# Hybrid gMLP and linear-attention layer on one core: the sample's attention in scaled two-byte halves, keys turned by DMA, states held at chunk ends, z and q/k weight steps and output steps moved a slot

## The chip, the core and the metric

The kernel runs on one core of a Trainium2 chip. Its engines are TensorE (PE, matmuls, with PEld for the loading of weights), VectorE (DVE), ScalarE (ACT), GpSimd (POOL) and SyncE (SP, here the queue that issues the DMAs). Each engine works through its own instructions in the order in which the program wrote them, and waits for the others through semaphores. The metric is device time in microseconds (us) of one launch; lower is better.

## The reference, cut to what matters

Two sequences, a prompt of 512 tokens and a sample of 2048, go through the same layer of width 1024. The part that this change touches is `gla_direction`, called once forward and once on the flipped sequence:

```python
h = rmsnorm(x, norm_pre)
u_a, v_a, z_a, q_b, k_b, v_b, z_b, lr_f, lr_b = split(h @ w_in)
out_a = spatial_gating(gelu(u_a), gelu(v_a), w_sp, b_sp, g_v_a) * silu(z_a)
# per direction, in chunks: g = log_sigmoid(lr @ w_gk + b_gk) / 16
bcum = cumsum(g, axis=2); b_last = bcum[:, :, -1:]
q_in, k_in = q * exp(bcum), k * exp(-bcum)
scores  = where(mask, einsum('bnchd,bnjhd->bnhcj', q_in, k_in), 0)
o_intra = einsum('bnhcj,bnjhe->bnche', scores, v)
chunk_kv = einsum('bnjhd,bnjhe->bnhde', k * exp(b_last - bcum), v)
state = exp(b_last) * state + chunk_kv            # scanned over the chunks
o_inter = q_in @ state_before
out_b = rmsnorm(o_fwd + o_bwd, g_norm_b) * silu(z_b)
y = x + rmsnorm(concat(out_a, out_b) @ w_out, norm_post)
```

The kernel uses chunks of 128 tokens; "chunk g" below is one of 20 such chunks, 0 to 3 of the prompt and 4 to 19 of the sample.

## The kernel before

Tokens are taken in five **blocks** of 512: block 0 is the prompt, blocks 1 to 4 the sample. A block is a row of **slots**. Each slot issues one projection of the block's normed input `hT` (a [128 x 512] result in one PSUM bank), and around it the steps of other generators whose turn it is. A projection is 24 matmuls, since input and weights are split into a high and a low float16 half and three of the four products are kept. In a sample block the slots are 0 to 3 `pv`, 4 to 7 `pzb`, 8 to 11 `pvb`, 12 to 15 `pqk` (columns 0, 2, 1, 3, so two of q and two of k), and 16 to 23 `pu` and `pz` in turn. In block 0 `pv` is done earlier, and slots 0 to 3 are `pzb`, 4 to 7 `pvb`, 8 to 11 `pu`, 12 to 15 `pqk`, 16 to 19 `pz`. After block 4 comes the **output stage**: for each of 20 row tiles two groups `py` of 24 matmuls with `w_out` and one small group `oi` (q times the state).

The program's order is final: nothing reorders it. In `slot`, the steps come in this order: the projections' readers (`mains`), weight steps named in `pre`, `early`, `aux` (the generators that a table adds at a slot), then the slot's own projection, then what was put into `late` (small matmuls). The PSUM pool `pj` of the projections has two banks, so the projection of slot s+2 waits until everything that reads the result of slot s is done.

What the change and the prediction name:

- **Weights** come as float32 `raw_*` and are split by `split_k`: ACT writes the high half, DVE the low half. For `w_z` four steps of two splits stand in block 0. Before them `g_wprep` takes a bound: two transposes on PE (`bank_z <- ident, m_z`), a DVE maximum `m_z`, and a small matmul with a row of ones (L191) that gives it to all partitions.
- **Next block's input**: `g_xprep` loads 128 rows `x`, squares them on ACT (L119), writes high half on ACT (L138) and low half on DVE (L140) and turns both by DMA into `hT` (L129). Its x and xs tiles share two buffers.
- **Gates**: `g_gates` makes the decay factors `QE` and `KE` with DVE scans (L576), a subtraction on each of POOL and DVE (L582, L584), a copy `ab` (L586, L587) and the exponentials on ACT.
- **v**: `g_vb` evacuates `pvb` with one ACT copy (L475). **q, k**: `g_qk` multiplies `pqk` into `QE` and `KE` with four DVE instructions.
- **Attention of a chunk**: `g_gla` computes scores `X` (forward) and `Y` (backward), merges them into `pr`, turns the keys into `kt` (on PE as `ktr` for chunks 0 to 3, 18, 19, else with 16 32-wide DVE transposes), and then `kv = kt^T v` and `o = pr^T v`, four float32 matmuls each. The forward state `U` is carried here.
- **Output steps**: `g_out` (called as `out_step(t)`) loads a row tile `L` of scratch, carries the backward state `U`, does `oi`, normalizes and splits into `OT`. `g_wout` loads and splits a piece of `w_out`.

Of the kernel before, what the change touches and what calls it, by code (L numbers as in the profile page):

```python
# [16 lines left out]
P = 128  # L17
# [3 lines left out]
NB = 5  # L21
# [10 lines left out]
OS = 2.0 ** 14  # L32


@with_exitstack
def tile_hybrid_gmlp_gla(ctx: ExitStack, tc: tile.TileContext, x_prompt, x_sample, norm_pre, w_in,
# [195 lines left out]
    def g_wprep(name):  # L232
# [126 lines left out]
    cols = cp.tile([P, 48], F32, name="cols")  # L359
# [182 lines left out]
    def g_gates(b):  # L542
# [64 lines left out]


    def decay_row(rows, g):
        n = rows.stop - rows.start  # L610
        return wst[rows, g, :].rearrange("p (h o) -> p h o", o=1).to_broadcast([n, H, P])

    PE_TR = (0, 1, 2, 3, 18, 19)

    def g_gla(b, i):
        g = 4 * b + i
        first = g in (0, 4)
        f, r = slice(0, 64), slice(64, 128)
# [4 lines left out]
        on_pe = g in PE_TR  # L623
        tr = pt.tile([P, H, P], F32, name=f"ktr{g}", tag="tr") if on_pe else None

        def k_transpose(q):
            d = slice(32 * q, 32 * q + 32)
            for c in range(4):
                nc.vector.transpose(out=kt[32 * c:32 * c + 32, :, d],  # L629
                                    in_=KE[b][d, :, i * P + 32 * c:i * P + 32 * c + 32])  # L630

        def mm():
            for h in range(H):
                nc.tensor.matmul(X[:, h, :], lhsT=KE[b][f, h, tk], rhs=QE[b][f, h, tk], start=True, stop=True)  # L634
                nc.tensor.matmul(Y[:, h, :], lhsT=KE[b][r, h, tk], rhs=QE[b][r, h, tk], start=True, stop=True)
            if on_pe:
                for h in range(H):
                    nc.tensor.transpose(tr[:, h, :], KE[b][:, h, tk], ident)
# [8 lines left out]
        if on_pe:  # L647
            nc.scalar.activation(kt, tr, AF.Copy)
        else:
            k_transpose(2)  # L650
            k_transpose(3)
# [9 lines left out]
        def kv_mm():  # L661
            for h in range(H):
# [488 lines left out]
```

## Time and profile before

| what | value |
|---|---|
| three runs | 976.3, 976.66 and 977.02 us; median 976.66 |
| the profiled execution | 976.77 us, of which the span of the trace is 975.1 |
| PE busy | 958.1 us, 98% of the span |
| DVE, ACT, POOL busy | 575.8 (59%), 417.9 (43%), 212.4 (22%) |

An engine's busy time is the union of its instructions. PE's matmuls overlap one another, so what a group of them costs is read from the start of its first to the start of what comes next, and not from the duration shown. The granted clock is full in every slice of the page.

### The profile page before, as it was taken

To read this page: it belongs to the slowest core of one execution; us is meant where nothing else is said; L and a number is where in the kernel's file an instruction comes from. 1 tells how busy PE (TensorE), PEld (TensorE's weight loads), DVE (VectorE), ACT (ScalarE), POOL (GpSimd) and SP (SyncE) were. 2 spreads that over 40 slices of the span, in tenths; PEclk is the share of its full clock that TensorE was granted. 3 is DMA by queue.
4 is the path that set the end of the run, shared out by engine and by line. 5 is a ranking of instruction groups with operands and counts; after the bars stand their busy time and mean duration, and the time that the engine had idled before them with its cause. 6 is when DMAs were issued, how large, how long until landed. Compare 5 with 4: busy or idle time off the path is not lost. (4 is left out here: it accounts for less than half of the span.)

```text
span 975.1 us, 14265 instructions
## 1 busy us (share of the span) xinstructions
PE 958.1 (98%) x5485; PEld 504.8 (52%) x5485; DVE 575.8 (59%) x1105; ACT 417.9 (43%) x792; POOL 212.4 (22%) x258
## 2 busy tenths in 40 slices
PE   8999999999999999999999999999999999999997
PEld 7744446544465544456444556444556555555454
DVE  6765864456756645755655667564665655565553
ACT  6778743535224363224453242343144444344341
POOL 1030203312021312011311112221022332222220
PEclk9999999999999999999999999999999999999999
DMA  9612134232433121333121331021416788767842
GB/s 322 229 68 84 24 106 121 86 97 44 97 108 109 44 87 44 87 119 105 50 74 44 108 120 66 33 76 66 151 66 202 223 263 252 221 221 228 251 158 97
DMA packets 113668, 120.71 MB, mean 124 GB/s; under 512 B 62784, under 2 KB 86208, under 8 KB 111040
## 3 DMA queue, kind: packets, MB, share of 16 engines
q1 hardware_dynamic: 113600, 119.80, 39.6%
q8 instruction: 43, 0.70, 0.3%
q14 instruction: 25, 0.20, 0.1%
HBM read 69.44 MB, written 36.70 MB: 109 GB/s over the span
## 5 line engine op out<-in xcount | busy, mean ns | idle before, releaser
L372 PEld LDWEIGHTS <-hT 128*128 128x128 f16 x1344 | 130.3, 98 | 159.1 <-issue 5.6
L836 PE MATMUL py<-wo,OT 128*128 128x512 f16 (+1 forms) x960 | 207.9, 376 | 0.0
L836 PEld LDWEIGHTS <-OT 128*128 128x128 f16 x984 | 96.3, 98 | 106.9
L372 PE MATMUL pzb<-w_zb,hT 128*128 128x512 f16 x480 | 106.6, 379 | 1.2 <-DVE tb L466 1.2
L382 PE MATMUL pz<-hT,w_z 128*128 128x512 f16 x480 | 107.0, 379 | 0.1
L382 PE MATMUL pu<-hT,w_u 128*128 128x512 f16 x480 | 106.6, 379 | 0.0
L372 PE MATMUL pvb<-w_vb,hT 128*128 128x512 f16 x480 | 104.9, 379 | 1.0 <-DVE tb L466 1.0
L382 PE MATMUL pqk<-hT,w_qk 128*128 128x512 f16 x480 | 104.8, 379 | 0.0
L629 DVE STREAM_TRANSPOSE kt<-KE 32x128 f32<-32x128 f32 x224 | 67.8, 303 | 34.4 <-PE kv L663 31.4
L372 PE MATMUL pv<-w_v,hT 128*128 128x512 f16 x384 | 84.5, 379 | 0.4 <-ACT vf L398 0.4
L382 PEld LDWEIGHTS <-w_u 128*128 128x128 f16 x480 | 46.9, 98 | 56.4
L382 PEld LDWEIGHTS <-w_qk 128*128 128x128 f16 x480 | 46.8, 98 | 56.0
L441 POOL TENSOR_TENSOR th<-th,gu 128x512 f32<-128x512 f32 x20 | 32.7, 1637 | 195.8 <-DVE th L440 195.8
L382 PEld LDWEIGHTS <-w_z 128*128 128x128 f16 x480 | 45.7, 98 | 54.2 <-issue 0.2
L455 ACT ACTIVATE th<-t 128x512 f32<-128x512 f32 x20 | 12.6, 630 | 132.2 <-DVE t L454 132.2
L855 DVE TENSOR_TENSOR y<-py,npost 128x512 f32<-128x512 f32 (+1 forms) x40 | 27.4, 685 | 70.7 <-PE py L836 60.6
L852 ACT ACTIVATE junk<-py 128x512 f16<-128x512 f32 (+1 forms) x40 | 23.7, 591 | 85.8 <-DVE y L855 84.6
L466 DVE SCALAR_TENSOR_TENSOR tb<-tb,pzb 128x512 f32<-128x512 f32 x20 | 13.7, 686 | 56.9 <-ACT tb L465 56.9
L582 POOL TENSOR_TENSOR KE<-QE 64x1024 f32<-64x1024 f32 x10 | 32.1, 3209 | 63.3 <-DVE QE L576 40.4
L486 DVE SCALAR_TENSOR_TENSOR QE<-pqk,ev_qk,QE 64x512 f32<-64x512 f32 x40 | 30.0, 749 | 26.0 <-PE pqk L382 24.3
L119 ACT ACTIVATE xs<-x 128x1024 f16<-128x1024 f32 x16 | 16.8, 1051 | 64.5 <-DMA x<-in_x_sample_dram 29.1
L646 DVE COPY_PREDICATED pr<-jlec,X 128x512 f32<-128x512 int32 x20 | 14.6, 730 | 40.6 <-ACT pr L645 40.5
(307 smaller groups left out, 1352.1 us busy)
## 6 DMA issues: line engine op xcount, KB each, us to landing
L<-scr SPq DMA_DIRECT2D x20, 1280.0 KB, 6.7
out_dram<-y SPq DMA_DIRECT2D x19, 512.0 KB, 7.4
x<-in_x_sample_dram SPq DMA_DIRECT2D x16, 512.0 KB, 4.0
xres<-in_x_sample_dram SPq DMA_DIRECT2D x16, 512.0 KB, 8.2
scr<-tb SPq DMA_DIRECT2D x20, 256.0 KB, 2.0
scr<-QE SPq DMA_DIRECT2D x20, 256.0 KB, 3.1
scr<-t SPq DMA_DIRECT2D x20, 256.0 KB, 2.4
scr<-S SPq DMA_DIRECT2D x20, 256.0 KB, 2.0
```

The costliest lines, as they stand in the source:

```text
L119: nc.scalar.activation(junk, xt, AF.Square, accum_out=ms)
L372: nc.tensor.matmul(ps, lhsT=hT[b][:, k, a, i * P:(i + 1) * P], rhs=w[:, k, c, :], start=(n == 0), stop=(n == 3 * KC - 1))
L382: nc.tensor.matmul(ps, lhsT=w[:, k, c, col:col + P], rhs=hT[b][:, k, a, :], start=(n == 0), stop=(n == 3 * KC - 1))
L441: nc.gpsimd.tensor_tensor(t, t, gus[b, h], op=ALU.mult)
L466: nc.vector.scalar_tensor_tensor(th, th, 1.0, ps, op0=ALU.add, op1=ALU.mult)
L486: nc.vector.scalar_tensor_tensor(o, ps[64 * hh:64 * hh + 64, :], s[64 * d:64 * d + 64], o, op0=ALU.mult, op1=ALU.mult)
L582: nc.gpsimd.tensor_tensor(Mv[64:128, h:h + 2], Av[64:128, h:h + 2, :, ::-1], mid[64:128, h:h + 2].to_broadcast([64, 2, 4, P]), op=ALU.subt ...
L629: nc.vector.transpose(out=kt[32 * c:32 * c + 32, :, d], in_=KE[b][d, :, i * P + 32 * c:i * P + 32 * c + 32])
L646: nc.vector.copy_predicated(pr, C["jmask"], X)
L836: nc.tensor.matmul(bank[:, cs], lhsT=OT[:, k, a, :], rhs=wo[n][:, k, c, cs], start=(m == 0), stop=(m == 3 * KC - 1))
L852: nc.scalar.activation(junk[:, cs], pss[j][:, cs], AF.Square, accum_out=ms[:, n + j:n + j + 1])
L855: nc.vector.tensor_tensor(y[:, n * 512:(n + 1) * 512][:, cs], pss[j][:, cs], npost[n][:, cs], op=ALU.mult)
```

## The change

- For the sample's chunks (4 to 19) `vb`, the keys and the masked scores are kept as a high and a low float16 half, and `kv` and `o` become three float16 matmuls per head (24 per chunk in place of 8 float32 ones).
- The keys of a chunk are first brought to the chunk's end (`kb`, on POOL), split (ACT and DVE), and turned by two DMA transposes on SP. The DVE and PE transposes of these chunks go.
- The scores get a scale per block: `g_qk` squares `pqk` on ACT, and a new `g_scores` sums this over partitions with two PE transposes and a matmul with ones (`bank_s`).
- `vb` is written by ACT (high) and by DVE (low), both from PSUM.
- States are held at chunk ends: one more POOL multiplication per chunk, and one (`um`) per row tile of the output stage for 15 tiles.
- In block 0 the four `w_z` steps go from slots 12 to 15 into slots 13 to 16, and one step of `w_z`'s bound from slot 11 to 12. The bound of `w_qk` is taken in two halves.
- The four `w_out` pieces of block 3 go to block 4, slots 5, 6, 12, 13, and the other four from slots 12 to 15 to 14 to 17. The output steps of block 4 are in other slots.

The diff, cut to its core:

```diff
@@ g_vb
+        if b > 0:
+            if i == 0:
+                vb[b] = bp.tile([P, 4, 2, 512], F16, name=f"vb{b}", tag="big8")
+            hi = vb[b][:, i, 0, :]
+            nc.scalar.activation(hi, ps, AF.Copy, scale=KS)
+            nc.vector.scalar_tensor_tensor(vb[b][:, i, 1, :], ps, KS, hi, op0=ALU.mult, op1=ALU.subtract)
+            return
@@ g_qk
+        if b > 0:
+            sq = tp.tile([P, BT], F32, name=f"sqk{b}_{c}", tag="S")
+            nc.scalar.activation(sq, ps, AF.Square, scale=SQ, accum_out=sqk[:, c:c + 1])
+def g_scores(b):
+        m = sp.tile([P, 2], F32, name=f"msc{b}", tag="s_msc", bufs=1)
+        nc.vector.tensor_reduce(m, sqk.rearrange("p (a c) -> p a c", a=2), axis=AX.X, op=ALU.add)
+        bank = pt.tile([P, 512], F32, name=f"bank_s{b}", tag="tr")
...
+                nc.tensor.transpose(bank[0:1, j * P:(j + 1) * P], m[:, j:j + 1], ident)
...
+        late.append(lambda: nc.tensor.matmul(bank[:, 256:258], lhsT=ones1, rhs=m2, start=True, stop=True))
@@ g_gla, sample chunks
+        nc.gpsimd.tensor_tensor(kb.rearrange("p (h t) -> p h t", t=P), KE[b][:, :, tk],
+                                spread(ab[:, 1], all_p, g), op=ALU.mult)
...
+        nc.scalar.activation(prh, Y, AF.Copy)
+        nc.scalar.activation(kb16[:, 0, :], kb, AF.Copy)
+        nc.vector.copy_predicated(prh, C["jmask"], X)
+        nc.vector.tensor_tensor(kb16[:, 1, :], kb, kb16[:, 0, :], op=ALU.subtract)
+        for a in range(2):
+            nc.sync.dma_start_transpose(out=kt16[:, a, :].rearrange("p (h d) -> p h d", d=P), in_=kb16[:, a, :])
...
+        nc.scalar.activation(pr16[:, 0, :], pr, AF.Copy, scale=s)
+        nc.vector.scalar_tensor_tensor(pr16[:, 1, :], pr, s, pr16[:, 0, :], op0=ALU.mult, op1=ALU.subtract)
...
+            for out, w in ((kv, kt16), (o, pr16)):
+                for h in range(H):
+                    hs = slice(h * P, (h + 1) * P)
+                    for n, (a, c) in enumerate(((0, 0), (0, 1), (1, 0))):
+                        nc.tensor.matmul(out[:, h, :], lhsT=w[:, a, hs], rhs=vb[b][:, i, c, hs],
+                                         start=(n == 0), stop=(n == 2))
@@ g_out
+            if b > 0:
+                mid = tp.tile([P, H, P], F32, name=f"um{g}", tag="ot")
+                nc.gpsimd.tensor_tensor(mid[r], U[r], to_mid(r, g), op=ALU.mult)
@@ block 0
-    tiny = {0: ["vb"], 1: ["vb"], 2: ["u"], 3: ["u"], 5: ["qk", "sp"], 6: ["qk", "sp"], 10: ["z"], 11: ["z"]}
-    pre = {2: [("vb", 4)], 3: [("vb", 5)], 12: [("z", 2)], 13: [("z", 2)], 14: [("z", 2)], 15: [("z", 2)]}
+    tiny = {0: ["vb"], 1: ["vb"], 2: ["u"], 3: ["u"], 5: ["qk", "sp"], 6: ["qk", "sp"], 10: ["z"], 12: ["z"]}
+    pre = {2: [("vb", 4)], 3: [("vb", 5)], 13: [("z", 2)], 14: [("z", 2)], 15: [("z", 2)], 16: [("z", 2)]}
@@ blocks 1 to 4
+        at(16, g_scores(b))
...
-            for s, piece in zip((19, 20, 21, 22), wo_pieces):
-                at(s, g_wout(*piece))
...
-            for s, piece in zip((12, 13, 14, 15), wo_pieces[4:]):
+            for s, piece in zip((5, 6, 12, 13, 14, 15, 16, 17), wo_pieces):
```

Two places show how the order of instructions moves. The number behind a name is a running number of the tile. The first place is ACT at the end of block 0, from the decay exponentials on: `w_z` are the high halves of the z weights, two per row, and `xs_1`, `xs_2` are rows of the next block's input. Before:

```order
L594 ACTIVATE KE_971<-KE_971 128x2048
L596 ACTIVATE ab<-ab 128x2x16
L218 ACTIVATE w_z<-raw_z,nps_z 128x512 x2
L119 ACTIVATE xs_1_1314,xms_1_1315<-x_1_1277 128x1024
L218 ACTIVATE w_z<-raw_z,nps_z 128x512 x2
L138 ACTIVATE xs_1_1314<-x_1_1277,xms_1_1315 128x1024
L218 ACTIVATE w_z<-raw_z,nps_z 128x512 x2
L119 ACTIVATE xs_2_1391,xms_2_1392<-x_2_1353 128x1024
L138 ACTIVATE xs_2_1391<-x_2_1353,xms_2_1392 128x1024
```

And now:

```order
L617 ACTIVATE KE_974<-KE_974 128x2048
L619 ACTIVATE ab<-ab 128x2x16
L220 ACTIVATE w_z<-raw_z,nps_z 128x512 x2
L121 ACTIVATE xs_1_1313,xms_1_1314<-x_1_1266 128x1024
L220 ACTIVATE w_z<-raw_z,nps_z 128x512 x2
L140 ACTIVATE xs_1_1313<-x_1_1266,xms_1_1314 128x1024
L220 ACTIVATE w_z<-raw_z,nps_z 128x512 x2
L121 ACTIVATE xs_2_1390,xms_2_1391<-x_2_1352 128x1024
L220 ACTIVATE w_z<-raw_z,nps_z 128x512 x2
L140 ACTIVATE xs_2_1390<-x_2_1352,xms_2_1391 128x1024
```

The last pair of splits, rows 6 and 7 of the eight slices of `w_z`, stood ahead of the square of `xs_2` and now stands behind it.

The second place is DVE in block 2 while PE does the four `pvb` projections; `tb_3` belongs to the last `pzb`, `KE`, `QE` and `ab` to the gates. Before:

```order
L466 SCALAR_TENSOR_TENSOR tb_3_3348<-tb_3_3348,pzb_3_3322 128x512
L575 TENSOR_TENSOR KE_3203<-QE_3202,KE_3203 128x1024
L576 SCALAR_TENSOR_TENSOR QE_3202<-smask,KE_3203 128x1024
L575 TENSOR_TENSOR KE_3203<-QE_3202,KE_3203 128x1024
L576 SCALAR_TENSOR_TENSOR QE_3202<-smask,KE_3203 128x1024
L584 TENSOR_TENSOR KE_3203<-QE_3202 64x2048
L586 COPY ab<-QE_3202 128x4x4
L587 TENSOR_TENSOR ab<-QE_3202 128x4x4
L140 SCALAR_TENSOR_TENSOR xs_1_3317<-x_1_3285,xms_1_3318,xs_1_3317 128x1024
```

And now:

```order
L598 TENSOR_TENSOR KE_3267<-QE_3266,KE_3267 128x1024
L599 SCALAR_TENSOR_TENSOR QE_3266<-smask,KE_3267 128x1024
L491 SCALAR_TENSOR_TENSOR vb_3444<-pvb_0_3418,vb_3444 128x512
L598 TENSOR_TENSOR KE_3267<-QE_3266,KE_3267 128x1024
L599 SCALAR_TENSOR_TENSOR QE_3266<-smask,KE_3267 128x1024
L607 TENSOR_TENSOR KE_3267<-QE_3266 64x2048
L609 COPY ab<-QE_3266 128x4x4
L610 TENSOR_TENSOR ab<-QE_3266 128x4x4
L142 SCALAR_TENSOR_TENSOR xs_1_3381<-x_1_3349,xms_1_3382,xs_1_3381 128x1024
L491 SCALAR_TENSOR_TENSOR vb_3444<-pvb_1_3457,vb_3444 128x512
L491 SCALAR_TENSOR_TENSOR vb_3444<-pvb_2_3485,vb_3444 128x512
L491 SCALAR_TENSOR_TENSOR vb_3444<-pvb_3_3516,vb_3444 128x512
```

The low half of the first `pvb` is read between the two scans, and that of the second only behind the whole gate chain and the input's low half. Block 3 has the same order; in block 4 there is no `xs_1`; in block 1 `vb` of the first three stands ahead of the second scan.

## Rows read from the trace of the kernel before

**Rows 1.** The page, busy time (share) x instructions of each engine.
```profile
PE 958.1 (98%) x5485; PEld 504.8 (52%) x5485; DVE 575.8 (59%) x1105; ACT 417.9 (43%) x792; POOL 212.4 (22%) x258
```

**Rows 2.** Waits of PE: who waited for whom, us in total, times, longest.
```profile
PE oi L784 <- ACT S L674: 0.7, 1, 0.7
...
PE pv L372 <- ACT vf L398: 0.4, 1, 0.4
```

**Rows 3.** Timeline of PE, one chunk of block 1: start, duration, instruction, count.
```profile
274.83 0.83 PE L447 MATMUL sv<-wspT,va 128*128 128x128 f16 x12
275.50 1.11 PE L663 MATMUL kv<-vb,kt 128*128 128x128 f32 x8
...
277.44 0.37 PE L634 MATMUL X<-QE,KE 64*128 64x128 f32 x1
```

**Rows 4.** PE's groups by line: busy us, mean ns, idle before.
```profile
L638 PE MATMUL ktr<-ident,KE 128*128 128x128 f32 x24 | 3.9, 286 | 0.0
```

**Rows 5.** Timeline of PE, end of block 0; brackets hold idle time and what ended it.
```profile
113.49 0.38 PE L191 MATMUL bank_z<-m_z,ones 1*128 1x1 f32 x2 [1.60 <-DVE m_z L190]
113.80 20.89 PE L382 MATMUL pqk<-hT,w_qk 128*128 128x512 f16 x96
134.53 5.34 PE L382 MATMUL pz<-hT,w_z 128*128 128x512 f16 x24
```

**Rows 6.** Timeline of ACT, end of block 0.
```profile
127.70 1.32 ACT L218 ACTIVATE w_z<-raw_z,nps_z 128x512 f16<-128x512 f32 x2
141.70 1.06 ACT L119 ACTIVATE xs<-x 128x1024 f16<-128x1024 f32 x1 [12.67 <-DMA hT<-xs]
```

**Rows 7.** Timeline of DVE, end of block 0.
```profile
132.62 1.41 DVE L219 SCALAR_TENSOR_TENSOR w_z<-raw_z,nps_z,w_z 128x512 f16<-128x512 f32 x2
133.95 1.28 DVE L140 SCALAR_TENSOR_TENSOR xs<-x,xms,xs 128x1024 f16<-128x1024 f32 x1
```

**Rows 8.** Timelines of PE, POOL and DVE, the `pvb` slots of block 2.
```profile
358.55 19.80 PE L372 MATMUL pvb<-w_vb,hT 128*128 128x512 f16 x91
...
369.82 4.01 POOL L582 TENSOR_TENSOR KE<-QE 64x1024 f32<-64x1024 f32 x1 [2.23 <-DVE QE L576]
...
371.98 1.89 DVE L586 COPY ab<-QE 128x16 f32<-128x16 f32 x1
373.79 0.18 DVE L587 TENSOR_TENSOR ab<-QE 128x16 f32<-128x16 f32 x1
373.89 1.27 DVE L140 SCALAR_TENSOR_TENSOR xs<-x,xms,xs 128x1024 f16<-128x1024 f32 x1
```

**Rows 9.** Timelines of PE and DVE, the `pvb` slots of block 4.
```profile
643.63 20.67 PE L372 MATMUL pvb<-w_vb,hT 128*128 128x512 f16 x95
...
658.64 0.18 DVE L587 TENSOR_TENSOR ab<-QE 128x16 f32<-128x16 f32 x1
```

**Rows 10.** Timelines of DVE, ACT and PE, block 1, `pvb` and `pqk` slots.
```profile
226.30 1.23 DVE L575 TENSOR_TENSOR KE<-QE,KE 128x1024 f32<-128x1024 f32 x1 [2.51 <-ACT QE L570]
...
227.22 0.69 ACT L475 ACTIVATE vb<-pvb,ev_vb 128x512 f32<-128x512 f32 x1 [0.94 <-PE pvb L372]
...
237.38 14.84 PE L382 MATMUL pqk<-hT,w_qk 128*128 128x512 f16 x68
...
240.51 1.91 ACT L591 ACTIVATE QE<-KE 128x2048 f32<-128x2048 f32 x1
```

**Rows 11.** Timelines of POOL and DVE, one row tile of the output stage.
```profile
835.18 0.30 POOL L796 TENSOR_SCALAR oms<-oms,cols 128x4 f32<-128x4 f32 x1
...
835.85 0.69 DVE L855 TENSOR_TENSOR y<-py,npost 128x512 f32<-128x512 f32 x1 [2.02 <-PE py L836]
...
838.72 0.74 DVE L807 SCALAR_TENSOR_TENSOR OT<-L,cols,OT 128x512 f16<-128x512 f32 x1
...
841.03 0.69 DVE L855 TENSOR_TENSOR y<-py,npost 128x512 f32<-128x512 f32 x1 [1.57 <-PE py L836]
```

**Rows 12.** One line of the trace: POOL's multiplication of `U` by a decay row.
```profile
L657 POOL TENSOR_TENSOR S<-U,wst x18: 1029/1032/1082, 172.0 to 745.9; 64x512 f32<-64x512 f32 x18
```

More of the change, by code (lines that the diff above doesn't have):

```diff
@@ L32 @@
 OS = 2.0 ** 14
+KS = 2.0 ** -18
+SQ = 2.0 ** -17
 @with_exitstack
@@ L243, in g_wprep @@
             m1 = sp.tile([P, 1], F32, name=f"m1_{name}", tag="s_m1w", bufs=2)
-            nc.scalar.activation(w[:, :, 0, :], r, AF.Abs, accum_out=m1)
-            nc.scalar.activation(m1, m1, AF.Identity, scale=anp1, bias=least)
+            if name == "qk":
+                m1a = sp.tile([P, 1], F32, name=f"m1a_{name}", tag="s_m12", bufs=1)
+                nc.scalar.activation(w[:, 0:4, 0, :], r[:, 0:4, :], AF.Abs, accum_out=m1a)
+                nc.scalar.activation(m1a, m1a, AF.Identity, scale=anp1, bias=least)
+                yield
+                nc.scalar.activation(w[:, 4:8, 0, :], r[:, 4:8, :], AF.Abs, accum_out=m1)
+                nc.scalar.activation(m1, m1, AF.Identity, scale=anp1, bias=m1a)
+            else:
+                nc.scalar.activation(w[:, :, 0, :], r, AF.Abs, accum_out=m1)
+                nc.scalar.activation(m1, m1, AF.Identity, scale=anp1, bias=least)
             yield
@@ L622, in g_gla @@
         kt = tp.tile([P, H, P], F32, name=f"kt{g}", tag="kt")
[L623 to L630, printed above, removed]
+        tr = pt.tile([P, H, P], F32, name=f"ktr{g}", tag="tr")
         def mm():
+            score_mm(b, i, X, Y)
             for h in range(H):
[L634 to L638, printed above, removed]
+                nc.tensor.transpose(tr[:, h, :], KE[b][:, h, i * P:(i + 1) * P], ident)
         late.append(mm)
-        if not on_pe:
-            k_transpose(0)
-            k_transpose(1)
         yield
@@ L646, in g_gla @@
         nc.vector.copy_predicated(pr, C["jmask"], X)
[L647 to L651, printed above, removed]
+        nc.scalar.activation(kt, tr, AF.Copy)
         yield
@@ L661, in kv_mm @@
         def kv_mm():
-            for h in range(H):
-                nc.tensor.matmul(kv[:, h, :], lhsT=kt[:, h, :], rhs=vb[b][:, i, h * P:(h + 1) * P],
-                                 start=True, stop=True)
-            for h in range(H):
-                nc.tensor.matmul(o[:, h, :], lhsT=pr[:, h, :], rhs=vb[b][:, i, h * P:(h + 1) * P],
-                                 start=True, stop=True)
+            for out, w in ((kv, kt), (o, pr)):
+                for h in range(H):
+                    nc.tensor.matmul(out[:, h, :], lhsT=w[:, h, :], rhs=vb[b][:, i, h * P:(h + 1) * P],
+                                     start=True, stop=True)
         late.append(kv_mm)
@@ L676, in g_gla, with turn @@
         nc.scalar.activation(ob, o, AF.Copy)
+        yield
+        nc.sync.dma_start(out=scr[b][:, i, 3, :], in_=S)
+        nc.sync.dma_start(out=scr[b][:, i, 0, :], in_=ob)
+    def g_scores(b):
+        m = sp.tile([P, 2], F32, name=f"msc{b}", tag="s_msc", bufs=1)
+        nc.vector.tensor_reduce(m, sqk.rearrange("p (a c) -> p a c", a=2), axis=AX.X, op=ALU.add)
+        bank = pt.tile([P, 512], F32, name=f"bank_s{b}", tag="tr")
+        def turn():
+            for j in range(2):
+                nc.tensor.transpose(bank[0:1, j * P:(j + 1) * P], m[:, j:j + 1], ident)
+        late.append(turn)
+        yield
+        m2 = sp.tile([1, 2], F32, name=f"ms2{b}", tag="s_m21", bufs=2)
+        nc.vector.tensor_reduce(m2, bank[0:1, 0:2 * P].rearrange("o (n p) -> o n p", p=P), axis=AX.X, op=ALU.add)
+        late.append(lambda: nc.tensor.matmul(bank[:, 256:258], lhsT=ones1, rhs=m2, start=True, stop=True))
+        yield
+        nc.vector.tensor_scalar(m, bank[:, 256:258], 1e-12, None, op0=ALU.max)
+        nc.gpsimd.tensor_tensor(m, m, neghalf[:, 0:2], op=ALU.pow)
+        s = sS[:, b % 2, 0:1]
+        nc.vector.tensor_scalar(s, m[:, 0:1], m[:, 1:2], qinv, op0=ALU.mult, op1=ALU.mult)
+        nc.vector.tensor_scalar(s.bitcast(I32), s.bitcast(I32), 0x7F800000, None, op0=ALU.bitwise_and)
+        i = sS[:, b % 2, 1:2]
+        nc.vector.reciprocal(i, s)
+        nc.vector.tensor_scalar(i, i, kap, None, op0=ALU.mult)
```

96 lines of the change are left out of this document (74 added, 22 removed).

## The prediction

> **What bounds the kernel now.** I read the page first: PE is busy for 958.1 of 975.1 us, DVE for 59%, ACT for 43% [rows 1]. PE's busy time can mislead, since its matmuls overlap, so I read next for whom PE waits. Apart from the start-up of the first 75 us these are three short places: 1.60 us before `bank_z` [rows 5], 0.7 before `oi` and 0.4 before a `pv` [rows 2]. So PE runs through its program nearly without a gap, and two things alone move the end: PE time that an edit takes away or adds, and a wait that it makes or removes on PE. Relief of another engine is worth nothing, so the 224 DVE transposes that go are not in the sum. For the same reason a small new job on DVE or ACT is dear if PE needs its result on time. PE needs most of them soon: `pj` has two banks, so a projection can begin only when the readers of the one two slots back are done.
>
> The sum is made against the profiled execution, 976.77 us; the median of the runs is 976.66, so 0.1 is taken off at the end.
>
> **What PE gains.** *Chunks.* In a chunk the eight matmuls of `kv` and `o` cost 277.44 − 275.50 = 1.94 us from start to start, 16 PE records, since each float32 matmul leaves two. Nearest to the new ones is `sv`: float16, the same 128 columns, 12 in 275.50 − 274.83 = 0.67, that is 56 ns each [rows 3]. 24 of them are 1.34, and with 0.09 for the change of kind behind them 1.43. 16 chunks × 0.51 = **−8.1**.
> The Trainium skill, "FP8 and Floating Point Precision", section TensorE Precision Notes, says that true float32 takes four passes of PE. By it the saving would be one pass in four, 8 × 56 ns a chunk, an estimate of 7.2 in all; the rows give 0.9 more, and they decide.
>
> *Turned keys.* The `ktr` transposes of chunks 18 and 19 go. Six chunks have them, 24 records, 3.9 us busy [rows 4]; 2/6 is 1.3, less some overlap: **−1.1**.
>
> *Waits.* The 0.7 before `oi` [rows 2] and a shorter one at the next step go, since `oi` now has another slot behind `pz`: **−0.8**. The 0.4 before `pv` at the start of block 4 [rows 2] comes behind `w_out` splits that leave block 3: **−0.4**. Together **−10.4**; block 0 is apart.
>
> **What PE pays in block 0.** Today `bank_z` waits 1.60 us for DVE [rows 5]; a `pqk` now stands ahead of it and covers that. Four `pqk` of 5.18 then lead to `pz`, 134.53 before. This gain can't be kept. In the order of ACT the last pair of `w_z` splits (k = 6 and 7 of 8) now stands behind the square of `xs_2`. That square started at 141.70 after 12.67 idle, released by the DMA that turns `xs_1` [rows 6], which itself follows DVE's low half at 133.95 + 1.28 [rows 7]. It does so again, because what stands ahead of it on DVE begins and ends at the same times. In before nothing on PE wanted ACT then; the splits were out at 127.70 [rows 6]. After it, `pz` reaches k = 6 at its 19th matmul, about 133.5 + 18 × 0.216 = 137.4, and waits: 141.70 + 1.06 + 0.2 for the square's accumulator, + 0.66 for one high half [rows 6] = 143.6; then two low halves on DVE at 0.7 each [rows 7], 145.0; the last matmuls end at about 145.2. Before, this `pz` ended at 134.53 + 5.18 = 139.7. So block 0 loses 145.2 − 139.7 = **+5.5**, with the 1.6 already counted back. It falls to −1.6 if the pair were in time, and can be 6.3 if the DMA lands a little later.
>
> **What PE pays for `bank_s`.** Two transposes, each about the 0.12 of one record in [rows 3], and two records with ones, 113.80 − 113.49 = 0.31 [rows 5]: 0.55, four blocks: **+2.2** (up to 2.8 with changes of kind).
>
> **What PE pays for the low half of `vb`.** Today `pvb` is read by ACT alone, and ACT has time. The low half is DVE's, 0.69 like any 128x512 from PSUM [rows 11], and it frees the bank.
> *Blocks 2 and 3.* DVE is busy without a gap until 373.89 + 1.27 = 375.16 [rows 8], and the order puts the low half of the second `pvb` behind all of it. The fourth `pvb` wants that bank at 358.55 + 3 × 5.18 = 374.09 [rows 8]. If nothing ahead moves, it starts at 375.16 + 0.69 + 0.1, a wait of 1.9. The low half of the first `pvb` stands ahead too, 0.69 more, unless the scan behind it was waiting for POOL anyway: 2.6 or, with friction, 3.2. I take 2.6, since the chain has only this one place where a wait could swallow it: **+5.2** for two blocks (3.7 to 6.4). Block 3 repeats the rows 141.9 us later.
> *Block 4.* No `xs_1`; the chain ends at 658.82, the bank is wanted at 643.63 + 15.54 = 659.17 [rows 9]. 658.82 + 0.69 + 0.69 + 0.1 = 660.3, a wait of 1.1; two `w_out` splits that now stand ahead of the gates on ACT can push it to 2.2: **+1.5** (0.4 to 2.2).
> *Block 1.* Three low halves stand ahead of the last scan, and the second waits for ACT's high half at 227.22 + 0.69, while the first scan's input was begun at 226.30 [rows 10]: the chain is 227.91 + 0.69 − 226.30 = 2.3 later, and with the third low half 3.0. The exponential of `QE`, at 240.51 + 1.91 before [rows 10], ends at 245.4 then; behind it DVE has 3.0 of `pqk` work and the square of `pqk` stands on ACT. The third `pqk` wants the first one's bank at 237.38 + 2 × 5.18 = 247.7 [rows 10], and gets it at 248.5 to 250.7. **+2.8** (1.0 to 3.5).
>
> **What I cost at nothing.** The DMA transposes of the keys: they have about 1.2 slots, over 6 us, and the matmuls that need them come a pair of slots later. If they took 2 us more than that, each chunk would pay. POOL's `kb`, ACT's and DVE's halves in a chunk: two slots of 5.18 and the small matmuls are some 13.5 us, and each engine gets under 4 more. The scale of the first chunk's scores goes through POOL, DVE and ACT just before `o` needs it: **+0.5** for all blocks (0 to 2).
> The output stage: `um` costs 1.03 like its neighbour [rows 12], stands behind POOL's work that ends at 835.48, and DVE's addition to `U` waits for it: 836.6 + 0.7 = 837.3, so the DVE job of 835.85 is 1.45 late. From the end of this chain, 838.72 + 0.74 = 839.46, DVE was free until 841.03 [rows 11], 1.57. It just fits, **0**, and 3 at most over 15 tiles.
> The Trainium skill, "GPSIMD Engine Reference", section 8 (Key points), says that GpSimd and VectorE contend for their way to SBUF when VectorE has two SBUF inputs or runs in its faster mode. The trace agrees: a copy of 16 columns took 1.89 and ended with POOL's subtraction, where the next instruction of that size took 0.18 [rows 8].
>
> **Sum.** −8.1 − 1.1 − 0.8 − 0.4 + 5.5 + 2.2 + 5.2 + 1.5 + 2.8 + 0.5 = **+7.3**. 976.77 + 7.3 − 0.1 = **984.0 us**.
>
> **Rivals.**
> *Faster, the low halves of `vb` are hidden.* If the gate chain on DVE ran 2.6 us earlier in each sample block, the banks would be free on time; the 9.5 go, and the time is 974.5. For it: `xs_1` need not be late, and POOL's part of the chain varies. Against: DVE shows no gap there to close [rows 8]. It decides where the chain's end comes before 373.3 in block 2. 0.10.
> *The pair of `w_z` comes in time.* Without the wait in block 0 the sum is 7.1 lower, 976.9: within 0.2%. For it: only one DMA holds the square. Against: that DMA follows DVE work that the change leaves where it was. 0.07.
> *The output stage is paced by DVE and POOL.* If `um` takes 1.2 to 1.3 beside other work, each tile is 0.1 to 0.2 late: +1.5 to +3, 986.5. Against: DVE waits while `um` runs, so nothing contends. 0.15.
> *As summed.* 0.68.
>
> The lower bounds of all terms give −10.4 + 5.5 + 2.2 + 3.7 + 0.4 + 1.0 = +2.4, 979; the upper ones −9.5 + 6.3 + 2.8 + 6.4 + 2.2 + 3.5 + 2 + 3 = +16.7, 993. Not all ends come together, so I cut the top at 990 and go down to 976.5, which takes in the second rival; below lies the first, 0.10, above another 0.08. A measurement of this kernel can tell about 0.2%, 2 us, from no change: faster is below 974.7 (the first rival, 0.10), the same 974.7 to 978.6 (0.07), slower the rest (0.83).
>
> **What would show it.** In the new trace: no wait at `bank_z`, but one inside the first `pz` of block 0, about 6 us, ended by ACT or DVE with `w_z`; `X` of chunk 0 near 145.3. A wait of 2 to 3 us before the fourth `pvb` of blocks 2 and 3, shorter in 4, ended by DVE's `vb`; in block 1 one before `pqk`. `kv` to `X` 1.4 us. `bank_s` 0.5. No wait at the first `oi` steps. Output tiles every 11.25 us as before, with `um` at 1.03. The prediction is wrong if the pair of `w_z` finds ACT free at 137 or if PE passes the fourth `pvb` unhindered; it is too low if `oi` or `py` begins to wait in the output stage, or `o` for its scaled scores.

## The result, and the profile after

The changed kernel takes 998.83 us (median of 5 runs, 996.7 to 1002.2) against 976.66 before: ratio 1.0231, interval 1.0209 to 1.0252. It is slower, as forecast, but by 22 us where 7.3 were summed, and outside the range of 976.5 to 990. The profiled execution is the fastest of the five, 996.70, so the trace explains 19.9 us against the 976.77 of before.

PE is again the engine to look at. These are its waits in the changed kernel: who waited for whom, us in total, times, longest. [rows 2] are the lines of before that answer to them.

```profile
PE pvb L385 <- DVE vb L491: 6.0, 3, 2.0
PE pz L395 <- ACT w_z L220: 5.7, 1, 5.7
PE oi L885 <- ACT L L879: 3.2, 14, 0.7
PE py L937 <- DMA OT<-L: 2.5, 3, 1.0
PE pqk L395 <- DVE QE L510: 1.9, 1, 1.9
...
PE pv L385 <- ACT vf L411: 1.4, 3, 0.5
...
PE py L937 <- ACT junk L953: 0.9, 1, 0.9
...
PE oi L885 <- ACT S L771: 0.7, 1, 0.7
```

The first, second and fifth line are the waits that the sum had. The third and fourth stand in the output stage and at its start, where the sum had nothing. How much later PE is than before, read from the start of the same instruction in both traces, shows it stage by stage:

| up to | before | after | later | in this stage | in the sum |
|---|---|---|---|---|---|
| second `pz` of block 0 | 141.39 | 147.41 | 6.0 | +6.0 | +5.5 |
| first `pv` of block 2 | 321.32 | 327.36 | 6.0 | 0.0 | +1.4 |
| first `pv` of block 3 | 463.21 | 470.80 | 7.6 | +1.6 | +1.2 |
| first `pv` of block 4 | 605.74 | 614.96 | 9.2 | +1.6 | +1.2 |
| last `sv` of block 4 | 748.09 | 759.53 | 11.4 | +2.2 | −2.2 |
| third full row tile's `oi` | 784.58 | 798.38 | 13.8 | +2.4 | 0 |
| last row tile's `oi` | 942.09 | 961.99 | 19.9 | +6.1 | 0 |

The last column spreads the terms of the sum over the stages. Up to block 3 the two columns agree within 1.4; from the last block on they are 12.9 apart. In the row of the last `sv`, 1.8 are waits of the first `py`, which stands ahead of it.

**Block 0.** The timeline of PE and of ACT at its end, beside [rows 5, 6]:

```profile
132.24 4.05 PE L395 MATMUL pz<-hT,w_z 128*128 128x512 f16 x18
141.95 2.74 PE L395 MATMUL pz<-hT,w_z 128*128 128x512 f16 x6 [5.66 <-ACT w_z L220]
```
```profile
140.13 1.06 ACT L121 ACTIVATE xs<-x 128x1024 f16<-128x1024 f32 x1 [12.75 <-DMA hT<-xs]
...
141.19 1.32 ACT L220 ACTIVATE w_z<-raw_z,nps_z 128x512 f16<-128x512 f32 x2
```

18 matmuls of `pz` run, the 19th waits 5.66 us. ACT has been idle for 12.75 us with the split next but one in its queue. Two things were not in the sum. The first came ahead of the wait: this one of before, in the start-up, is gone.

```profile
73.03 5.34 PE L372 MATMUL pvb<-w_vb,hT 128*128 128x512 f16 x24 [1.05 <-DVE tb L466]
```

PE comes to block 0's `pu` 1.27 us earlier, and what follows shifts with it: the square began at 140.13 and not at 141.70 as the sum had it. All versions of the changed kernel have such a head start, 0.9 to 1.4, and the kernel before with the z steps alone has 0.1, so another part of the change gives it; which one was not tested. The second thing came behind the wait: the windows of the same stretch (us, busy time and instructions of PE, PEld, DVE, ACT, POOL, granted clock, DMA share, GB/s).

```profile
130.00:140.00 10.00, 6.29 (x30) 2.65 (x27) 7.10 (x9) 0.00 (x0) 0.00 (x0) 1.00 0.51 125
140.00:150.00 10.00, 8.05 (x39) 4.35 (x40) 4.04 (x5) 5.29 (x8) 2.99 (x3) 0.66 0.42 126
```

After the idle PE gets a mean clock of 0.66 over these 10 us, that is, about 6.8 of them at the lower of its two levels (1.2 in place of 2.4 GHz), the first part still inside the wait. The last six matmuls and the chunk behind them take 147.41 − 141.95 = 5.46 us to the next `pz`. Before, they took 2.97, from 134.53 + 18 × 0.216 = 138.42 to 141.39. So the lower clock cost 2.5.

**A chunk.** `kv` to `X` is now 285.01 − 283.58 = 1.43 us, 1.94 before [rows 3]: the term of the sum to the hundredth.

```profile
283.58 0.83 PE L763 MATMUL kv<-vb,work 128*128 128x128 f16 x12
284.25 0.83 PE L763 MATMUL o<-vb,work 128*128 128x128 f16 x12
285.01 0.37 PE L643 MATMUL X<-QE,KE 64*128 64x128 f32 x1
```

**Block 2.** DVE and PE in the `pvb` slots, beside [rows 8]:

```profile
379.08 1.89 DVE L609 COPY ab<-QE 128x16 f32<-128x16 f32 x1
380.89 0.18 DVE L610 TENSOR_TENSOR ab<-QE 128x16 f32<-128x16 f32 x1
380.99 1.27 DVE L142 SCALAR_TENSOR_TENSOR xs<-x,xms,xs 128x1024 f16<-128x1024 f32 x1
382.18 0.68 DVE L491 SCALAR_TENSOR_TENSOR vb<-pvb,vb 128x512 f16<-128x512 f32 x1
```
```profile
382.91 5.34 PE L385 MATMUL pvb<-w_vb,hT 128*128 128x512 f16 x24 [1.98 <-DVE vb L491]
```

The fourth `pvb` starts 0.05 us after the low half of the second ends. The wait is 1.98 us, and from start to start PE loses 2.14: between the 1.9 that the sum gave as its lower bound and the 2.6 that it took. The chain on DVE from the gates' first step (`L598`) to the input's low half is 13.16 us in place of 12.73, 0.43 more, although the first low half of `vb`, 0.66, is new in it. Beside POOL's first subtraction DVE loses time in both kernels: before, the second scan took 3.89 there and not 2.29; now the step ahead of that scan takes 2.63 and not 1.20.

**A row tile of the output stage.** All engines but PE's weight loads, beside [rows 11]:

```profile
917.59 0.75 DVE L908 SCALAR_TENSOR_TENSOR OT<-L,cols,OT 128x512 f16<-128x512 f32 x1
...
918.32 0.69 DVE L956 TENSOR_TENSOR y<-py,npost 128x512 f32<-128x512 f32 x1
...
918.47 1.16 POOL L907 TENSOR_TENSOR L<-L 128x512 f16<-128x512 f32 x1 [1.13 <-ACT L L906]
918.93 1.91 DVE L980 SCALAR_TENSOR_TENSOR y<-y,yr,xres 128x512 f32<-128x512 f32 x2
...
920.77 0.67 DVE L890 TENSOR_TENSOR L<-L,oi 128x512 f32<-128x512 f32 x1
...
924.62 1.04 POOL L874 TENSOR_TENSOR um<-U,ab 64x512 f32<-64x512 f32 x1
925.69 0.69 DVE L878 TENSOR_TENSOR U<-ub,L 64x512 f32<-64x512 f32 x1 [3.53 <-POOL um L874]
926.41 0.69 DVE L956 TENSOR_TENSOR y<-py,npost 128x512 f32<-128x512 f32 x1
...
927.09 1.16 PE L885 MATMUL oi<-L 128*128 128x128 f32 x8 [0.17 <-ACT L L879]
```

`um` takes the 1.04 that was forecast, and a wait of DVE of 3.53 us ends with it. But `L956`, which was free to wait for PE at 841.03 in before, now follows `L908` without a gap and PE's `oi` waits for this chain. DVE, ACT and POOL run a closed loop, and it sets the pace: 11.69 us a tile in place of 11.25. The row shows a wait of 0.17, less than the loss: from start to start of `oi` a tile is 0.44 longer.

The place where the loop grew is DVE's pair `L980` beside POOL's `L907`. The tile before this one has it with another length, and the loop with the same:

```profile
906.78 1.16 POOL L907 TENSOR_TENSOR L<-L 128x512 f16<-128x512 f32 x1 [1.12 <-ACT L L906]
906.86 0.69 DVE L956 TENSOR_TENSOR y<-py,npost 128x512 f32<-128x512 f32 x1 [0.21 <-DMA out_dram<-y]
907.47 1.68 DVE L980 SCALAR_TENSOR_TENSOR y<-y,yr,xres 128x512 f32<-128x512 f32 x2
```

The pair ends 1.21 us after POOL's subtraction does, here (909.15 and 907.94) and there (920.84 and 919.63). It is so in 12 of the 14 steady tiles, whenever in the subtraction the pair began, so it takes 1.50 to 1.99 in them. In the other two a wait of 0.63 and 0.66 for the store of an earlier `y` had put the pair at the subtraction's end, and it took 1.41 and 1.40.

### The profile page after: what moved, and what is told of

Read it like the earlier page. It is cut to its first block, busy times and chain, and to the rows that moved or that the text cites. A ratio compares the mean times of both kernels' runs of the same rounds, so it can differ in the third digit from the quotient of the medians.

```text
span 995.0 us, 14560 instructions
## 1 busy us (share of the span) xinstructions
PE 960.3 (97%) x5621; PEld 497.5 (50%) x5621; DVE 548.8 (55%) x959; ACT 448.4 (45%) x857; POOL 267.7 (27%) x308
## 5 line engine op out<-in xcount | busy, mean ns | idle before, releaser
L385 PEld LDWEIGHTS <-hT 128*128 128x128 f16 x1344 | 130.0, 98 | 165.6 <-issue 12.2
L454 POOL TENSOR_TENSOR th<-th,gu 128x512 f32<-128x512 f32 x20 | 35.6, 1779 | 131.7 <-DVE th L453 124.1
L605 POOL TENSOR_TENSOR KE<-QE 64x1024 f32<-64x1024 f32 x10 | 29.6, 2962 | 66.0 <-DVE QE L599 46.9
L878 DVE TENSOR_TENSOR U<-ub,L 64x512 f32<-64x512 f32 x16 | 11.0, 689 | 60.6 <-POOL um L874 49.4
L125 POOL TENSOR_SCALAR xms<-xms 128x1 f32<-128x1 f32 x16 | 3.4, 211 | 141.5 <-ACT xs L121 141.1
L465 DVE SCALAR_TENSOR_TENSOR t<-sv,gv,bsp 128x512 f32<-128x512 f32 x20 | 15.0, 748 | 45.3 <-PE sv L460 38.8
L956 DVE TENSOR_TENSOR y<-py,npost 128x512 f32<-128x512 f32 (+1 forms) x40 | 27.3, 684 | 18.3 <-PE py L937 10.5
L894 ACT ACTIVATE sq<-L 128x128 f32<-128x128 f32 x80 | 23.7, 297 | 30.3 <-DVE L L890 30.3
```

Source lines behind the costliest of these rows:

```text
L385: nc.tensor.matmul(ps, lhsT=hT[b][:, k, a, i * P:(i + 1) * P], rhs=w[:, k, c, :], start=(n == 0), stop=(n == 3 * KC - 1))
L454: nc.gpsimd.tensor_tensor(t, t, gus[b, h], op=ALU.mult)
L465: nc.vector.scalar_tensor_tensor(t3, sv, C["gv"][:, h:h + 1], C["bsp"][:, h:h + 1, :].to_broadcast([P, 4, P]), op0=ALU.mult, op1=ALU.add)
L605: nc.gpsimd.tensor_tensor(Mv[64:128, h:h + 2], Av[64:128, h:h + 2, :, ::-1], mid[64:128, h:h + 2].to_broadcast([64, 2, 4, P]), op=ALU.subt ...
L878: nc.vector.tensor_tensor(U[r], tmp[r], kvb, op=ALU.add)
L894: nc.scalar.activation(sq[:, h, :], o[:, h, :], AF.Square, accum_out=ms[:, h:h + 1])
```

## The experiments

All times are medians; differences are against the changed kernel's 998.83, if nothing else is said. Its five runs lie 5.5 us apart, so a difference of 2 us or less, which four of the edits below give, is not clear of that spread, and there only the traces say what the edit did.

**um one tile ahead.** `um_next(g)` is the multiplication that the tile after g needs; it follows this tile's addition to `U`.

```diff
-            mid = tmp
-            if b > 0:
-                mid = tp.tile([P, H, P], F32, name=f"um{g}", tag="ot")
-                nc.gpsimd.tensor_tensor(mid[r], U[r], to_mid(r, g), op=ALU.mult)
+            mid = tmp if b == 0 else ums.pop(g)
...
+            if b > 0 and g != 4:
+                um_next(g)
```

> Edit: in the output stage the multiplication um of a row tile is issued on POOL one tile earlier, right behind the addition to U that it reads; nothing else. Theory A (the output stage is paced by a loop over DVE, ACT and POOL in which um, 1.04 us, stands between POOL's oms and DVE's addition to U): um leaves the loop, tiles come every 11.25 us again instead of 11.69, and the 0.17 waits of oi vanish: 14 x 0.44 = 6 us less than the changed kernel (998.8 median, profiled 996.7), about 991 profiled. Rival B (the extra 0.44 is the landing of the DMA transposes or DMA traffic of the longer states): um's place is indifferent, tiles stay at 11.69, time as the changed kernel.

993.95 us (ratio to before 1.0175, 1.016 to 1.019), 4.9 less. Tiles come every 11.25 us again (`oi` at 926.14 and 937.39), and `oi` waits for `um` no more. So theory A holds, and B falls. From its third full tile to its last `oi` this version takes 157.5 us, the changed kernel 163.6: 6.1 less.

**um twice.**

```diff
                 nc.gpsimd.tensor_tensor(mid[r], U[r], to_mid(r, g), op=ALU.mult)
+                nc.gpsimd.tensor_tensor(mid[r], U[r], to_mid(r, g), op=ALU.mult)
```

> Edit: um is computed twice in a row on POOL into the same tile (one copy too many, result unchanged). Theory A: the loop grows by the 1.05 us of one POOL multiplication, tiles come every 12.7 us, 15 x 1.05 = 15.8 us more than the changed kernel, about 1012 profiled. Rival B (DMA): POOL has idle time in each tile, so no more than 2 us.

1013.63 us, 14.8 more, where 15.8 were expected. PE's timeline has a tile each 12.79 us, 1.10 more than 11.69:

```profile
901.97 1.16 PE L886 MATMUL oi<-L 128*128 128x128 f32 x8 [1.27 <-ACT L L880]
902.96 10.52 PE L938 MATMUL py<-wo,OT 128*128 128x512 f16 x48
914.76 1.16 PE L886 MATMUL oi<-L 128*128 128x128 f32 x8 [1.28 <-ACT L L880]
```

Each microsecond put on POOL there is a microsecond of the kernel, although in the changed kernel POOL is busy for only 27% of the span.

**POOL's other work beside DVE.** This version leaves out the low half of the normalized attention output; ACT writes zeros in its place.

```diff
-        nc.gpsimd.tensor_tensor(ob[:, 1, :], L[:, 0, :], ob[:, 0, :], op=ALU.subtract)
+        nc.scalar.activation(ob[:, 1, :], L[:, 0, :], AF.Copy, scale=0.0)
```

> Edit: the changed kernel, with um where the change put it, but POOL's subtraction that makes the low half of the normalized attention output (1.16 us per tile) left out: ACT writes zeros there, so the low half of that part is missing from the result. In the changed kernel this subtraction runs beside DVE's y = y * r + xres, which took 1.91 us for two instructions against 1.40 before. Theory F (um alone would just have fitted; what lifts the loop over PE's 11.25 is that DVE's late instructions now run beside POOL's subtraction): the two take 1.4, the loop is 11.2, tiles come every 11.25 and oi does not wait: 5 to 6 us less than the changed kernel, 992 to 994. Theory A alone (um's 1.04 is the whole cost): tiles stay at 11.6 to 11.7.

996.97 us, 1.9 less, not the 5 to 6 of theory F. From the third full tile's `oi` to the last it takes 160.9 us, 2.7 less than the changed kernel's 163.6. DVE's pair takes 1.40 in every tile:

```profile
909.25 1.40 DVE L980 SCALAR_TENSOR_TENSOR y<-y,yr,xres 128x512 f32<-128x512 f32 x2
```

The loop then turns in 11.1 us in seven of 14 steady tiles (DVE's `L890` from tile to tile), below PE's 11.25, and in 11.3 and 11.4 in two more. In the other five it takes 11.9 to 12.2, since DVE waits 0.7 to 1.0 for the store of an earlier `y` to land:

```profile
863.07 0.69 DVE L956 TENSOR_TENSOR y<-py,npost 128x512 f32<-128x512 f32 x1 [0.98 <-DMA out_dram<-y]
```

So F is right about what POOL's subtraction costs a tile, and wrong that nothing else stood close behind it: a loop that just fits has no room for a late store. With `um` ahead DVE waits up to 3.4 us for such stores, and the tiles still come every 11.25.

**The z weight steps alone, in the kernel before.**

```diff
-    tiny = {..., 10: ["z"], 11: ["z"]}
-    pre = {..., 12: [("z", 2)], 13: [("z", 2)], 14: [("z", 2)], 15: [("z", 2)]}
+    tiny = {..., 10: ["z"], 12: ["z"]}
+    pre = {..., 13: [("z", 2)], 14: [("z", 2)], 15: [("z", 2)], 16: [("z", 2)]}
```

> Edit: the kernel before with one part of the change alone, the z weight steps of block 0 a slot later (bound 10 and 12, splits 13 to 16). Theory: the same wait of 5.5 us inside the first pz of block 0 as in the changed kernel, 1.6 gained before bank_z, 1 to 2 more lost to a lower granted clock behind the wait: 981 to 983. Rival (the wait is only seen because other parts of the change make ACT or DVE late there): within 1 us of 976.7.

983.36 us, 6.6 more than before (ratio 1.0068, 1.0051 to 1.0085). The wait is there without any other part of the change, and so is the lower clock, in the windows of this run:

```profile
140.00:150.00 10.00, 6.62 (x34) 3.63 (x35) 3.94 (x5) 5.27 (x8) 2.99 (x3) 0.66 0.51 133
```

PE is 1.2 us ahead of before at the first `pz`, mostly from `bank_z`, and 7.0 behind at the second: 5.95 of wait and about 2.2 of lower clock. By the third `pzb` of block 1 0.6 have come back. The 6.4 that are left stay the same to the end, and the profiled run is 6.4 longer.

**The z weight steps back, and packed closer, in the changed kernel.** The first takes the two lines above back; the second puts the splits into slots 13, 14 and 15 as three, three and two.

> Edit: the z weight steps of block 0 in the slots they had before the change (bound 10 and 11, splits 12 to 15); all else as changed. Theory: the 5.66 us inside the first pz go, and with them the stretch at a granted clock of 0.66 behind it; the 1.6 before bank_z come back: about 5 us less than the changed kernel. Rival (as with three splits a slot: DVE is late for the next pz by itself): no more than 3 us.

> Edit: the eight splits of the z weights in slots 13, 14, 15 as three, three and two, none in slot 16; all else as changed. Theory: the wait of 5.66 us inside the first pz of block 0 goes, since no split stands behind the square of xs_2; up to 1 us comes back before pz because the third low half delays the readers of pqk on DVE: 4.7 to 5.7 us less than the changed kernel. Rival: the wait is owed to DVE's low halves or to something else late there, and returns before pz or the next projection: less than 2 us gained.

996.85 (2.0 less) and 994.36 (4.5 less). In both the 5.66 are gone. With the closer packing 2.4 come back as waits for DVE (a `pqk` 1.1 in place of 0.5, two `pz` 0.3 and 1.5), against 1.0 expected. Of the old slots, PE is 5.4 earlier at the `pqk` of block 1 (247.9 for 253.3), as expected, and keeps it up to the fourth `pvb` of block 2. By its time alone the rival (no more than 3) would stand as well, but the trace shows where the gain went: behind the waits of 2 us in blocks 2 and 4 the granted clock is 0.83 over 10 us, which costs 1.7 each time and which the changed kernel's profile has not, and waits in the output stage take the rest.

**The input piece a slot later.**

```diff
-            for i, s in enumerate((1, 6, 11, 15)):
+            for i, s in enumerate((1, 7, 11, 15)):
```

> Edit: in blocks 1 to 3 the preparation of the second 128 rows of the next block starts at slot 7 in place of 6, so DVE's low half of them (1.27 us) stands behind the low half of the second pvb; all else as changed. Theory (the fourth pvb waits for DVE's low half of the second, which is behind the gate chain): the wait in blocks 2 and 3 falls from 1.98 by 1.27 to about 0.7, that of block 4, without such rows, stays at 2.0: 2.5 us less in all. Rival (POOL's subtraction, which DVE's copy waits out, or ACT's high half sets it): the wait stays within 0.3 of 1.98.

The waits of the fourth `pvb` fall from 1.98 to 0.02 in blocks 2 and 3 and stay at 2.01 in block 4: the place is right, and the piece held it for longer than DVE's 1.27. Its square on ACT had stood ahead of the copy of the last `pzb`; now that copy begins 0.26 us after the first `pvb` of block 2 in place of 1.28, and DVE's gate chain with it. Yet the whole is 997.56, only 1.3 less where 2.5 were expected: in block 1 a new wait of 0.5 before `pqk` opens, the one there grows to 2.05, and the granted clock behind it is 0.83 over 10 us, where the changed kernel's profile has 1.00.

**The output steps.** First the old table in the changed kernel, then the load of the second row tile a slot earlier.

```diff
-            for s, t in ((17, 0), (18, 0), (19, 0), (19, 1), (20, 0), (20, 1), (21, 1), (22, 1), (22, 0), (23, 0)):
+            for s, t in ((17, 0), (19, 0), (19, 1), (20, 0), (21, 0), (21, 1), (22, 0), (22, 1), (23, 0), (23, 1)):
```

> Edit: the table of output steps in block 4 as before the change; all else as changed. Theory C (the output stage begins late because the load of the second row tile now stands only one slot ahead of DVE's addition to U that reads it: DVE waited 5.67 us for that DMA at 732, and everything behind it, POOL's oms, the turning of OT and the loads of the next tiles on SP, came some 6 to 10 us late): that wait goes, the three waits of py at the start of the output stage (1.0, 0.75 and 0.7 for the turned OT, 0.9 for a bank) fall to under 1 us in all, 3 to 4 us less than the changed kernel. Rival D (POOL's extra multiplications per chunk and SP's extra key turns are what is late): the waits of py stay.

1006.68 us, 7.9 more. The waits of `py` for the turned `OT` do fall, from 2.5 to 0.7, so D is wrong. But C is wrong in its remedy: PE now waits in the middle of the last chunks.

```profile
PE oi L885 <- ACT S L771: 8.8, 2, 5.9
```

There ACT waits for DVE, DVE waits 7.12 us for a store of `t` (`DMA scr<-t`) to land, and POOL 5.71 for one of `S`.

```profile
733.75 0.75 DVE L465 SCALAR_TENSOR_TENSOR t<-sv,gv,bsp 128x512 f32<-128x512 f32 x1 [7.12 <-DMA scr<-t]
```

The key turns, the loads of the row tiles and these stores now share SP in the same slots, and the table that was good before is not good now. Which of them makes the stores late was not told apart.

```diff
-            ... (19, 0), (19, 1), (20, 0) ...
+            ... (18, 1), (19, 0), (20, 0) ...
```

> Edit: the changed kernel with the load of the second row tile at slot 18 in place of 19, nothing else. Theory C: DVE's wait of 5.67 us for it goes and the waits of py (1.0, 0.75, 0.9, 0.7) fall by 1 to 2.5 us in all. Rival E: no gain, or a wait of oi of several us. The output tiles stay at 11.69 us with either.

997.91, 0.9 less: DVE's wait of 5.67 us for that load is gone, the waits of `py` for the turned `OT` fall from 2.5 to 1.4, and `oi` waits 1.2 in place of 0.7. C has the right place and a small price; most of the gap at the start of the output stage was left.

**Versions with several edits.** The first joins `um` ahead, the old output steps, the old z slots, the later input piece in blocks 2 and 3, and the output scale of block 4 at slot 10. The second has the changed kernel's output steps and the scale at slot 13. The third adds the earlier load, the fourth the earlier turn of the first row tile, and the fifth moves two `w_out` pieces:

```diff
+            for s, t in ((17, 0), (18, 0), (18, 1), (19, 0), (20, 0), (20, 1), (21, 1), (21, 0), (22, 1), (22, 0)):
...
-            for s, piece in zip((5, 6, 12, 13, 14, 15, 16, 17), wo_pieces):
+            for s, piece in zip((10, 11, 12, 13, 14, 15, 16, 17), wo_pieces):
```

> Edit: five things at once in the changed kernel: um one tile ahead, the old table of output steps, the old z slots, the second input piece of blocks 2 and 3 a slot later (start 7), and the output scale in block 4 at slot 10 in place of 6. If the waits found are all that the change cost and they add up, 998.8 - 6 (um) - 4 (steps) - 5 (z) - 4 (vb of blocks 2 and 3) - 1.5 (vb of block 4) leaves 978, with 1 to 2 less for clock stretches that follow waits: 975 to 980, the time before. If they overlap or move elsewhere: over 984.

> Edit: the joined version, but with the changed kernel's own table of output steps, and the output scale in block 4 at slot 13. Theory: the two waits of oi (5.9 and 2.9) that the old table brought into the joined version go, and the clock stretches behind them; the three waits of py at the start of the output stage come back (2.5): about 986.6 - 9 - 3 + 3 = 977 to 979, the time before. Rival (the old table's waits were owed to the joined edits and not to the table): 984 or more.

> Edit: as the one with four edits, and the load of the second row tile at slot 18 in place of 19. Theory C (that load stands one slot ahead of its reader on DVE and lands 6.7 us after issue): DVE's wait of 5.67 us goes, POOL and SP behind it are on time, and the waits of py at the start of the output stage fall by 1 to 2.5 us: 975 to 977. Rival E (the DMA queues are full there: a load moved ahead makes the stores of t and S land late, and DVE or POOL waits for those): no gain, or a wait of oi of several us, as with the old table.

> Edit: as the one before, and the two last steps of the first row tile (its normalizing and its turning by DMA) at slots 21 and 22 in place of 22 and 23. Theory: the turned OT is there a slot pair earlier, the loads of the third and fourth tile are no longer queued behind it on SP, and py begins without a wait: 1 to 2 us less than with the load alone, 974 to 976. Rival E: as above, no gain.

> Edit: the best version so far (um ahead, old z slots, input piece of blocks 2 and 3 a slot later, output scale at slot 13, load and turning of the first row tiles earlier) and the first two w_out pieces at slots 10 and 11 in place of 5 and 6 of block 4. Theory: the split of 1.13 us that stood ahead of the last gate steps on ACT goes from there, the wait of the fourth pvb in block 4 falls from 1.13 to about 0: 1 us less, 975. Rival: the low halves of w_out, 1.3 us on DVE, now stand among the readers of pvb and pqk and a wait of the same size opens there: 976 or more.

| version | us | ratio to before (interval) |
|---|---|---|
| joined, old output steps | 986.63 | 1.0098 (1.0083 to 1.0113) |
| four edits | 980.44 | 1.0039 (1.0027 to 1.0052) |
| and the earlier load | 978.39 | 1.0018 (1.0009 to 1.0027) |
| and the earlier turn | 975.96 | 0.9990 (0.9981 to 0.9999) |
| and two `w_out` pieces later | 974.64 | 0.9980 (0.9971 to 0.9989) |

The first was forecast at 975 to 980 and missed by the old output steps' two waits of `oi`, 8.8 us. The next three came within 2 us of what was expected, the last within 0.4. Its wait of the fourth `pvb` in block 4 is gone, as expected. The last two lie below both kernels, the last by 2.2 us or 0.2% of the time before. What it still waits for most:

```profile
PE pv L385 <- ACT vf L411: 2.1, 3, 1.2
...
PE pqk L395 <- DVE QE L510: 1.9, 1, 1.9
```

## Why the prediction was wrong

**What held.** PE's program order bounds the kernel. The chunks gain 0.51 us each. The pair of `w_z` splits behind the square of `xs_2` makes PE wait inside the first `pz` of block 0: 5.66 measured, and shown by the z steps alone. That block 0 came out at +6.0 for +5.5 is in part luck: a head start of 1.3 and a lower clock that cost 2.5, neither in the sum, nearly cancel with smaller differences. The low half of `vb` frees the bank late: 1.98 for 2.6 in blocks 2 and 3, 2.0 for 1.5 in block 4, 1.9 for 2.8 in block 1. `bank_s` costs 0.62 a block for 0.55. The gains at `bank_z` and from the turned keys came.

**The step that failed** is the one on the output stage: "It just fits, **0**, and 3 at most over 15 tiles." It cost 6.1 in the steady tiles and 2.4 at their start. The pace was among the rivals (paced by DVE and POOL, 0.15), at +1.5 to +3 and from a slower `um`; `um` took its 1.04. The lateness of 1.45 us was laid against 1.57 us of free DVE, each with its duration from [rows 11]. But work that comes 1.45 us later stands beside other work. DVE's pair `L980`, 1.40 before, now begins while POOL subtracts, and ends 1.21 us after that subtraction in 12 of 14 tiles; where nothing else delays it, it takes 1.99. The 0.59 between is the difference of 11.69 and 11.10, and the experiment without POOL's subtraction showed the other end of it: 1.40 and a loop of 11.1 in half of the tiles. The store of `y`, which had its room in the same 1.57 us, is what kept the other tiles long there. With `um` out of the loop the 6.1 went whole.
The prediction quoted the rule that covers this, the Trainium skill, "GPSIMD Engine Reference", section 8 (Key points), on GpSimd and a VectorE instruction with two SBUF inputs, and found the trace in agreement. It then argued against the rival that "DVE waits while `um` runs, so nothing contends". That looked at the new instruction alone. The contention was between two old ones that the delay pushed together.

**What was missed besides.** The terms −0.8 and −0.4 for waits that go: one wait of `oi` (0.7) stayed, and `pv` waits 0.47 at the start of three blocks in place of 0.36 at one, so about 1 us was lost where 1.2 were to be gained. The lower clock behind a wait, 2.5 us in block 0, was in no term. The start of the output stage: `py` waits 3.4 us in all for the turned `OT` and for a bank. "The DMA transposes of the keys" were costed at nothing because no chunk waits for them, which holds; what SP has behind them, the load and turn of the first row tiles, was not looked at. SP's queue in the changed kernel, at the first turn of `OT` (`L912`):

```profile
750.86 2.58 SPq L743 DMA_TRANSPOSE work<-work  x2
753.49 2.56 SPq L912 DMA_TRANSPOSE OT<-L  x2
```

POOL had that `OT` ready at 750.91, and two key turns (`L743`) held the queue for 2.58 us ahead of it; the load of the second row tile, at 725.66, stands behind two others of 2.51. The first two waits of `py` are shorter than this, 1.02 and 0.75. The runs on the output steps show that place to be worth 4 to 5 us (980.44 to 975.96), and how tightly its DMAs, POOL and DVE are coupled (1006.68 with the old table). No run moves the key turns alone, so their part in it is read from this trace and not shown by an experiment.

**The rest of the median,** 2.1 us over the profiled run, is not in that trace. The five runs order by granted clock: 996.70 at 0.996, 997.78 and 998.83 at 0.995, 1000.98 at 0.992, 1002.2 at 0.990. So it is likely, though not shown for those runs, that they had stretches of lower clock that the profiled one had not; what such a stretch costs is seen below.

## What to carry to other kernels

A delay that fits into an engine's idle time is free only if the delayed work runs as fast at its new time: look what it will run beside, and add up the closed loop with those durations before writing zero. Where an instruction is moved in an in-order queue, ask not what it costs but what now stands ahead of it and what that waits for. A table of slots is tuned to one set of DMAs and queues; after the work in the slots changes, neither the old table nor a small step from it can be trusted without a trace.

## What the runs showed of the hardware that was not expected

A wait of PE can cost more than its length. After the 5.5 to 6 us of idle in block 0 the granted clock was below full in all eight profiles that had that wait: 0.66 to 0.69 over 10 us in six, 0.73 and 0.83 in the other two. After a wait of about 2 us before a fourth `pvb` it is sometimes lower and sometimes not: in 8 of 25 such waits in nine profiles, and PE then came 1.7 us later. These are windows of the changed kernel and of the one with `um` ahead, the same program up to there:

```profile
380.00:390.00 10.00, 8.02 (x38) 3.51 (x37) 4.32 (x7) 5.94 (x7) 0.93 (x1) 1.00 0.31 80
```
```profile
380.00:390.00 10.00, 8.02 (x30) 3.25 (x29) 4.06 (x5) 4.31 (x4) 1.45 (x1) 0.83 0.33 80
```

In the second PE did 30 matmuls in the same busy time instead of 38, and was 1.7 us later behind them (383.42 to 483.52 against 382.91 to 481.32). That such waits spread the runs is likely and not shown run by run: the changed kernel's lie 5.5 us apart, those of before 0.8, and those of the last version, with fewer waits, 1.6.

DVE did not merely run slower beside POOL. Of the 12 pairs `L980` in the changed kernel's steady tiles that began well within POOL's subtraction, and of 16 in the version with `um` twice, each had its first instruction end 0.55 us after the subtraction and its second 1.21 after it, however long before the end it had begun (0.29 to 0.79 us).
